# Mask and forget-gate sums built in DRAM during the projections, a reordered gate schedule, and new prices in the instruction planner

## The chip, the cores and the metric

The kernel runs on one core of a Trainium2 chip. The metric is the device time of one launch in microseconds (us). A profile of one execution gives the span of the program and the work of each engine: TensorE (PE, with its weight loads PEld), VectorE (DVE), ScalarE (ACT), GpSimd (POOL) and SyncE (SP), whose queue issues nearly all transfers.

## The reference

One layer of a hybrid encoder on a sequence of 1024 frames of 1024 channels, in float32. A token mixer with two parallel branches is followed by a gated feed-forward block; each has a residual sum and a layer norm.

```
proj = x @ w_in                # q,k,v,f of branch A; q,f,i,g of branch B; gate_a, gate_b
F    = cumsum(log_sigmoid(f_a + b_f))                    # per head, 8 heads of 64
s    = q.k / 8 + F[t] - F[s],  only keys s <= t
y_a  = softmax(s) @ v                                    # forgetting attention
y_b  = rms_norm(hgrn2(silu(q_b), f, i_b)) * sigmoid(g_b) # gated recurrence, 4 heads of 128
mix  = (sigmoid(gate_a) * (y_a @ w_pa) + sigmoid(gate_b) * (y_b @ w_pb)) @ w_o
x    = layer_norm(2**0.25 * x + mix)
out  = layer_norm(2**0.25 * x + (silu(g) * u) @ w_ff_out)   # u, g = x @ w_ff_in
```

The row constant F[t] drops out of the softmax; what attention adds to a row of scores is a term per key made from F, and a large number where a key lies ahead of the query.

## The kernel before, in words

**Arithmetic.** Every float32 product is made of three matmuls of 512 columns: each operand is split into a rounded high part (ScalarE, a copy to fp32r) and the rest as its low part (VectorE, a subtraction; `split`, line 463). The projections, gates and feed-forward products are Strassen products of seven in place of eight quarters.

**Stages.** First the values of both branches and the forget gates: `forget_gates` (627) and `forget_sums` (672) leave the gate sums, one row of 1024 numbers for each of 8 heads, in DRAM as `nf_d` (625). Then ten pairs of projections (`b_pair`, 829, for the recurrence; `qk_pair`, 814, for the queries and keys), whose weights go through the SBUF tile `box1` (594), two of its four slots for each pair in turn. Between them the recurrence of the four HGRN heads (`hgrn`, 1025). Then eight early parts of the merge gates (`gate_early`, 859: two of seven products, kept in DRAM as `part_d`; its weights in slots 0 and 1 of `box1`), eight heads of attention (`attention`, 913) and the eight late parts of the gates (`gate_late`, 870). After this come the branch projections, the output projection, and the feed-forward block.

**Attention.** A head h loads its queries and keys and two slots of `box1` (lines 922 to 925): one with the gate row on all 128 partitions, for blocks of keys fully behind the query, the other with the gate row plus the causal mask, for the blocks on the diagonal. This second slot is made in two transfers: SP loads the mask from the input, then GpSimd's queue adds the gate row to it with an accumulating DMA. Even heads use slots 2 and 3, odd heads 0 and 1. VectorE adds slot and scores and finds the row's minimum, ScalarE takes the exponential, GpSimd divides by the row sum (`pool.tensor_scalar`), TensorE transposes the blocks, they are split and multiplied with the values. The two halves of a head's result are added by another accumulating DMA of GpSimd's queue and stored to `ya_d`.

**Weights of the late gates.** Gate n takes its two raw weight tiles from the tags wr0 and wr1 (one buffer each) for even n, from the tag pf (four buffers) for odd n (line 1171). After the last gate, the branch projection loads its first weights, `wp0_0`, into wr0 and the next into wr1.

**The planner.** Nothing is issued in program order. Each call goes into `Plan` (line 62), which keeps its dependences and an estimated duration (`cost`, 145), and `schedule` (188) simulates the five queues: it always places the call that can start first and, among equals, that of the lowest rank. The steps listed in `ORDER` (34) give the first ranks, the dependences through shared tiles, and the order in which tiles of a tag are handed out. `improve` (371) repeats this 36 times, each time with ranks from the latest start that a backward pass finds (`latest`, 331), and keeps the order with the earliest simulated end. Each engine then issues its calls in that fixed order.

The prices: `LAT` is the delay in ns after which another engine sees a result, with 2400 for a transfer of SP; `OWN` the same on its own engine. A transfer of GpSimd's queue holds that engine for `SOFT` = 950 ns and lands `LANDS` + bytes / `RATE` later. A result that TensorE waits for gets `SLACK` ns on top (line 37). `MARGIN` = 1.06 stretches the durations of the other engines. Where a VectorE operation has two inputs in SBUF (`c[8]`), it is stretched while GpSimd is at work (line 268):

```
d += 0.7 * min(d, max(0.0, free["POOL"] - t))
```

`plan.behind` adds a dependence by hand: the calls recorded while it is set may not start ahead of the calls it names.

Of the kernel before, what the change touches and what calls it, by code (L numbers as in the profile page):

```python
# [7 lines left out]
F32 = mybir.dt.float32  # L8
# [4 lines left out]
ALU = mybir.AluOpType  # L13
# [3 lines left out]
P = 128  # L17
S = 1024
D = 1024
KC = D // P  # L20
NT = S // P
HA, DH = 8, 64
# [8 lines left out]
FIRST = 8  # L31
WARM = 7
ROUNDS = 36
ORDER = ("b10 00", "r0", "b20 21", "r0", "b11 01", "r0", "r0", "r0", "r0", "q0", "r1", "r1", "b12 02", "r1", "r1", "q1", "r1", "r1", "b22 23", "r2", "r2", "r2", "b13 03", "r2",
         "r2", "r2", "q2", "r3", "r3", "e0", "q3", "r3", "r3", "e1", "r3", "e2", "r3", "e3", "e4", "e5", "e6", "e7", "a0", "a1", "g0", "a2", "g1", "a3", "a4", "g2", "a5", "a6", "g3", "a7", "g4", "g5", "g6", "g7")
MARGIN = 1.06
SLACK = 400.0
SWITCH = 300.0
RING = 3
ALPHA = 2.0 ** 0.25  # L40
# [21 lines left out]
class Plan:  # L62

    LAT = {"PE": 197.0, "ACT": 131.0, "DVE": 128.0, "POOL": 66.0, "SP": 2400.0}
    OWN = {"PE": 0.0, "ACT": 0.0, "DVE": 127.0, "POOL": 60.0, "SP": 2400.0}
    SOFT, LANDS, RATE, SOONER = 950.0, 1950.0, 200.0, 1150.0
    TURN, STAY = 22.0, 300.0
    SETS = {AF.Exp: 0, AF.Ln: 0, AF.Sigmoid: 1, AF.Silu: 2}  # L70

# [73 lines left out]
    def cost(self, eng, method, outs, ins, kw):  # L145
        o = outs[0]
        n = o.free_size()
        psum = any(str(a.space).endswith("PSUM") for a in ins)
        if eng == "PE":
            dt = ins[0].dtype  # L150
            if method == "transpose":
                return 109.0
            if dt == F32:
                return 2 * max(112.0, n / 1.2 + 2)
            return n / 2.4 + 13.4 if n > 128 else 111.0
        if eng == "ACT":
            d = n / 1.2 + (52 if psum else 94) + 95 * (o.partition_size() == DH)
            if "accum_out" in kw:
                d += 93
            return d + 93 * sum(isinstance(kw.get(x), bass.AP) for x in ("scale", "bias"))  # L160
        if eng == "DVE":
            scal = sum(1 for a in ins if a.free_size() == 1 and n > 1)
            two = method in ("tensor_scalar", "tensor_copy") and not psum
            if method == "reciprocal":
                return 90.0
            if method == "tensor_tensor_scan":
                return n * 2.1 + 69
            if method == "copy_predicated":
                return n * 1.3 + 69
            if method == "bn_stats":  # L170
                n = ins[0].free_size()
            return n * (0.5208 if two else 1.0417) + 69 + 61 * min(scal, 2)
        if eng == "POOL":
            if method == "dma_start":
                return self.SOFT
            if method == "tensor_tensor" and kw.get("op") == ALU.pow:
                return 500 + 260 * n
            if method == "tensor_scalar":
                return n * 0.833 + 244
            return n * 2.35  # L180
        near = ins[0] if str(o.space).endswith("DRAM") else o
        rate = 235.0 if near.partition_size() == DH else 220.0 if tuple(ins[0].ap[0]) == (0, P) else 350.0
        return float(o.nbytes()) / rate
# [4 lines left out]
    def schedule(self, slack, wait):  # L188
# [12 lines left out]
        free = {q: 600.0 for q in self.queues}  # L201
# [19 lines left out]
        while done < len(calls):  # L221
            best = None
            for q, av in avail.items():
                for i in av:
                    t = max(free[q], ready[i])
                    ok = True
                    need = {}
                    for name in calls[i][6]:
# [10 lines left out]
                        t = max(t, sorted(slots[tag])[k][0] + 60)  # L239
# [3 lines left out]
                    if self.lands[i]:  # L243
                        t = max(t, ring[-RING])
                    if q == "SP":
                        t = max(t, under_way[-8])
# [4 lines left out]
                    r = self.rank[i]  # L251
# [6 lines left out]
            t, _, i, q = best  # L258
# [6 lines left out]
                narrow = self.narrow[i]  # L265
            if q == "DVE" and c[8]:

                d += 0.7 * min(d, max(0.0, free["POOL"] - t))
            if q == "SP":
                start = max(t + 100, dma_free)  # L270
                dma_free = start + d
# [138 lines left out]
def trunk(ctx: ExitStack, tc, a: dict, out: bass.AP):  # L410
    nc = tc.nc
    plan = Plan(tc)
# [19 lines left out]
    def take(tag, shape, name, dt=F32):  # L432
        return plan.tile(root, [P] + shape, dt, tag, name, BUFS[tag])
# [189 lines left out]


    nf_d = dram.tile([HA, S], F32, name="nf_d")

    def forget_gates():

# [200 lines left out]
    def b_pair(which, raws, banks):  # L829
        name = "b" + "".join(f"{i}{h}" for i, h in which)  # L830
        perm = which[0][0] < 2

        def put(b, hf, o, sv):
            bi, h = which[b]
            if b == 0 and hf:
                t = half("gt", f"{name}_o")
                act.activation(sv(t), o, AF.Sigmoid)
            elif bi == 0:
                t = o
                s = half("gt", f"{name}_s{hf}")  # L840
                act.activation(s, t, AF.Sigmoid)
                dve.tensor_mul(t, t, s)
            else:
                t = o
                act.activation(t, t, AF.Sigmoid)
            if bi == 1:
                act.activation(t, t, AF.Identity, scale=olb[:, h:h + 1], bias=lb[:, h:h + 1])
            if perm:
                sync.dma_start(b_d[bi, h].rearrange("p (c h t) -> p h c t", c=2, h=2)[:, hf],
                               t.rearrange("p (c t) -> p c t", c=2))  # L850
            else:
                sync.dma_start(b_d[bi, h, :, hs(hf)], t)

        strassen_pair(name, [a["w_b"][bi, h] for bi, h in which], raws, banks, perm, put)
# [58 lines left out]
    def attention(h):  # L913
        p, i = divmod(h, 2)
        me = slice(i * DH, (i + 1) * DH)
        if True:
# [4 lines left out]
            r = 2 - 2 * (h % 2)  # L921
            nfx = box1[:, r:r + 2, :].rearrange("p a (b t) -> p (a b) t", t=P)
            sync.dma_start(box1[:, r, :], nf_d[h].partition_broadcast(P))
            sync.dma_start(box1[:, r + 1, :], a["causal"])
            pool.dma_start(box1[:, r + 1, :], nf_d[h].partition_broadcast(P), accum_op=ALU.add)
            vhl = take("hl", [NT, 2, DH], f"vhl{h}", F32R)
            sync.dma_start(f(vhl), v_d[h])
            pr = []
# [96 lines left out]
    def hgrn(h, box):  # L1025
# [100 lines left out]
        for hf in range(2):  # L1126
# [20 lines left out]
            sync.dma_start(yb_d[h, :, hs(hf)], y)  # L1147
            yield

    rbox = take("v", [4, S], "rbox")  # L1150
    pairs, heads = 0, []
    for step in ORDER:
        kind, n = step[0], int(step[1])
        if kind in "bq":
            raws = [slot(box1, 2 * (pairs % 2) + i) for i in range(2)]
            banks = (("h", "h"), ("s", "s"))[pairs % 2]
            pairs += 1
            if kind == "q":
                qk_pair(n, raws, banks)
            else:  # L1160
                b_pair([(int(x[0]), int(x[1])) for x in step[1:].split()], raws, banks)
        elif kind == "e":
            gate_early(n, slot(box1, n % 2), "hs"[n % 2])
        elif kind == "r":
            if not heads or heads[-1][0] != n:
                heads.append((n, hgrn(n, rbox)))
            next(heads[-1][1])
        elif kind == "a":
            attention(n)
        else:  # L1170
            raws = [take(t, [KC, P], f"wg{n}_{i}") for i, t in enumerate((("wr0", "wr1"), ("pf", "pf"))[n % 2])]
            gate_late(n, raws, ("h", "h"))


# [748 lines left out]
```

## Time and profile before

| | |
|---|---|
| median of 3 runs | 1404.1 us (1402.64 to 1406.85) |
| the profiled execution's own time | 1403.85 us |
| its span in the profile | 1402.1 us |
| TensorE busy | 1387.0 us, 6578 matmuls |
| VectorE busy | 1154.1 us |
| ScalarE busy | 660.0 us |
| GpSimd busy | 113.8 us |
| TensorE clock granted, mean | 0.998 |
| DMA moved | 250.42 MB |

By time from the start of the span: the values and forget gates up to 87 us, projections with the HGRN heads to about 340, the early gates around 340 to 390, attention with the late gates to about 600, the branch projections to 640 and 680, the output projection to about 750, the feed-forward block from there.

A busy engine has an instruction under way; matmuls overlap in their pipeline, so one of 389 ns may follow the last after 227. A wait of TensorE shorter than the rest of the pipeline is therefore not seen as idle time. In the lists of waits a row says who waited for whose work, the total in us, how often, and the longest. In a timeline a row has its start, length, engine, line, operation, and in brackets the idle time before it and what ended it. All calls are issued from one line, 406, so work is told apart by the tiles that it writes and reads: `s` are attention's scores, `p` and `p_w` its weights, `pt`, `th`, `tl` the transposed block and its two parts, `pv` its result; `ge` and `gl_` belong to early and late gates, `T...h` and `T...l` are the two parts of a weight, `box` is `box1`, `rbox`, `hk`, `lp` belong to HGRN, `pps_` to the branch projections.

### The profile page before, as it was taken

The numbers are of one execution on the slowest core, as the hardware profiler recorded it, in microseconds if no ns is written. First come the engines' busy times: TensorE is split into PE (matmuls) and PEld (weight loads), VectorE is DVE, ScalarE is ACT, GpSimd is POOL, SyncE is SP. The second block draws the span as 40 slices with busy tenths as digits, with TensorE's granted clock in tenths as the row PEclk, the third lists the DMA queues.
The fourth block names the chain that finished last, engine by engine and source line by source line (L and its number), as shares of the span: only waits on it lengthen the run. The fifth ranks groups of instructions, "written<-read, shape, count | busy, mean of one in ns | idle before, by whom it ended". The sixth has DMA issues, their size and how long they took to land.

```text
span 1402.1 us, 19062 instructions
## 1 busy us (share of the span) xinstructions
PE 1387.0 (99%) x6578; PEld 1148.8 (82%) x6578; DVE 1154.1 (82%) x2026; ACT 660.0 (47%) x1207; POOL 113.8 (8%) x120
## 2 busy tenths in 40 slices
PE   9999999999999999999999999999999999999997
PEld 7788888888788888888887888888888888888886
DVE  8998797896498987888998889877766767999697
ACT  6545454444476776465549832233333334434430
POOL 0000001010143542000001000000000000000031
PEclk9999999999999999999999999999999999999999
DMA  7143344447897886556544636533233337977732
GB/s 273 37 177 125 108 141 151 135 136 235 275 327 236 286 240 207 178 177 222 197 147 143 208 111 224 171 120 100 99 98 110 113 113 237 337 243 231 267 133 75
DMA packets 103426, 250.42 MB, mean 179 GB/s; under 512 B 11665, under 2 KB 16913, under 8 KB 103329
## 3 DMA queue, kind: packets, MB, share of 16 engines
q1 hardware_dynamic: 100896, 242.91, 51.2%
q0 software_dynamic: 2432, 6.29, 2.5%
q8 instruction: 52, 0.85, 0.3%
q14 instruction: 46, 0.37, 0.1%
HBM read 182.77 MB, written 64.29 MB: 176 GB/s over the span
## 4 chain that ended last, share of the span: by engine, by line
PE 89%; DMA 6%; DVE 2%; ACT 1%; issue 1%; POOL 0%; SPq 0%; DVEq 0%; ACTq 0%
PE p L406 15%; PE fb L406 12%; PE fc L406 9%; PE gl_h L406 7%; PE fa L406 5%; PE b_h L406 4%; PE qk_s L406 4%; PE vx L406 4%; PE oa L406 3%; PE pps L406 3%; PE pv L406 2%; PE s L406 2%; PE ob L406 2%; PE vy L406 2%; PE pt L406 2%; PE lp L406 2%
## 5 line engine op out<-in xcount | busy, mean ns | idle before, releaser
L406 PE MATMUL p<-dp 128*128 128x512 f32 (+1 forms) x957 | 210.0, 382 | 0.0
L406 PEld LDWEIGHTS p<-dp 128*128 128x128 f32 x957 | 175.3, 188 | 34.8
L406 PE MATMUL fc<-xs,Tp 128*128 128x512 f32 x528 | 127.6, 389 | 0.0
L406 PE MATMUL fb<-xs,Tp 128*128 128x512 f32 x528 | 127.5, 389 | 0.0
L406 ACT CAST Tp<-t 128x512 fp32r<-128x512 f32 x88 | 54.5, 620 | 132.3 <-PE fb L406 59.9
L406 PEld LDWEIGHTS fc<-xs,Tp 128*128 128x128 f32 x528 | 99.1, 188 | 20.6
L406 PEld LDWEIGHTS fb<-xs,Tp 128*128 128x128 f32 x528 | 99.1, 188 | 20.6
L406 DVE TENSOR_TENSOR Tp<-t,Tp 128x512 fp32r<-128x512 f32 x88 | 60.6, 690 | 46.0 <-ACT Tp L406 45.5
L406 POOL TENSOR_TENSOR norm<-norm,few 128x1 f32<-128x1 f32 x16 | 23.4, 1464 | 796.8 <-DVE norm L406 781.7
L406 PE MATMUL fa<-x,Tp 128*128 128x512 f32 x336 | 80.9, 389 | 0.0
L406 PEld LDWEIGHTS fa<-x,Tp 128*128 128x128 f32 x336 | 63.1, 188 | 13.1
L406 ACT CAST dp<-dap 128x1024 fp32r<-128x1024 f32 (+1 forms) x42 | 40.9, 979 | 49.6 <-PE p L406 26.0
L406 DVE TENSOR_TENSOR tl<-pt,th 128x512 fp32r<-128x512 f32 (+1 forms) x96 | 52.5, 553 | 11.8 <-ACT th L406 9.6
L406 ACT CAST th<-pt 128x512 fp32r<-128x512 f32 (+1 forms) x96 | 45.6, 478 | 29.0 <-PE pt L406 24.2
L406 PE MATMUL fb<-x,Tp 128*128 128x512 f32 x240 | 57.6, 389 | 0.0
L406 DVE TENSOR_TENSOR dp<-dap,dp 128x1024 fp32r<-128x1024 f32 (+1 forms) x42 | 47.2, 1130 | 10.4 <-ACT dp L406 10.4
L406 PEld LDWEIGHTS fb<-x,Tp 128*128 128x128 f32 x240 | 45.0, 188 | 9.4
L406 DVE TENSOR_TENSOR u<-fb,p 128x512 f32<-128x512 f32 x40 | 27.6, 690 | 25.7 <-PE fb L406 25.7
L406 ACT CAST Tp<-wg_r 128x512 fp32r<-128x512 f32 x28 | 17.5, 623 | 48.1 <-PE fb L406 26.5
L406 POOL TENSOR_SCALAR p_w<-p_w,sums 128x640 f32<-128x640 f32 (+3 forms) x32 | 36.6, 1179 | 28.0 <-DVE sums L406 19.7
L406 PE MATMUL pv<-tl,vhl 128*128 128x512 f32 (+1 forms) x96 | 34.7, 365 | 1.3 <-DVE tl L406 1.3
L406 PE MATMUL pt<-ident,p_w 128*128 128x128 f32 x208 | 35.7, 274 | 0.0
(1657 smaller groups left out, 3672.0 us busy)
## 6 DMA issues: line engine op xcount, KB each, us to landing
dbp<-in_w_fo SPq DMA_DIRECT2D x45, 512.0 KB, 4.9
dap<-a_d SPq DMA_DIRECT2D x35, 512.0 KB, 4.4
wu_r<-in_w_ff SPq DMA_DIRECT2D x22, 512.0 KB, 3.7
wg_r<-in_w_ff SPq DMA_DIRECT2D x22, 512.0 KB, 3.9
a_d<-ar SPq DMA_DIRECT2D x42, 256.0 KB, 3.0
wop_r<-in_w_o SPq DMA_DIRECT2D x18, 512.0 KB, 4.0
a_d<-as SPq DMA_DIRECT2D x33, 256.0 KB, 3.4
qk_d<-qk SPq DMA_DIRECT2D x32, 256.0 KB, 3.3
```

The costliest lines, as they stand in the source:

```text
L406: getattr(q.engine, method)(*args, **kw)
```

## The change

Six edits go together.

1. A new DRAM tensor `nfc_d` holds gate row plus causal mask for each head. The new function `masked(h)` copies the mask to it inside DRAM on SP's queue, behind the last call recorded so far, and adds the gate row by an accumulating DMA of GpSimd's queue. It is called after each of the first eight projection pairs.
2. `attention` loads its second slot from `nfc_d` in one transfer; the mask load and the accumulating DMA of each head go.
3. In `ORDER`, head 0 (`a0`) stands ahead of the early gates `e6` and `e7`, and the late gate `g0` ahead of head 1. The rest of the list is the same.
4. The late gates swap their weight tags: even ones take pf, odd ones wr0 and wr1.
5. VectorE operations with two SBUF inputs are stretched by all of the time for which GpSimd is still busy. The masked copy of VectorE costs 2.4 ns an element in place of 1.3 where its innermost run is short or strided.
6. `SLACK` goes from 400 to 500 ns, SP's latency from 2400 to 2700, `LANDS` from 1950 to 4000, `RATE` from 200 to 150.

```
@@ -31,10 +31,9 @@
 FIRST = 8
 WARM = 7
 ROUNDS = 36
-ORDER = ("b10 00", "r0", "b20 21", "r0", "b11 01", "r0", "r0", "r0", "r0", "q0", "r1", "r1", "b12 02", "r1", "r1", "q1", "r1", "r1", "b22 23", "r2", "r2", "r2", "b13 03", "r2",
-         "r2", "r2", "q2", "r3", "r3", "e0", "q3", "r3", "r3", "e1", "r3", "e2", "r3", "e3", "e4", "e5", "e6", "e7", "a0", "a1", "g0", "a2", "g1", "a3", "a4", "g2", "a5", "a6", "g3", "a7", "g4", "g5", "g6", "g7")
+ORDER = ('b10 00', 'r0', 'b20 21', 'r0', 'b11 01', 'r0', 'r0', 'r0', 'r0', 'q0', 'r1', 'r1', 'b12 02', 'r1', 'r1', 'q1', 'r1', 'r1', 'b22 23', 'r2', 'r2', 'r2', 'b13 03', 'r2', 'r2', 'r2', 'q2', 'r3', 'r3', 'e0', 'q3', 'r3', 'r3', 'e1', 'r3', 'e2', 'r3', 'e3', 'e4', 'e5', 'a0', 'e6', 'e7', 'g0', 'a1', 'a2', 'g1', 'a3', 'a4', 'g2', 'a5', 'a6', 'g3', 'a7', 'g4', 'g5', 'g6', 'g7')
 MARGIN = 1.06
-SLACK = 400.0
+SLACK = 500.0
 SWITCH = 300.0
 RING = 3
 ALPHA = 2.0 ** 0.25
@@ -63,9 +62,9 @@
 
 
 
-    LAT = {"PE": 197.0, "ACT": 131.0, "DVE": 128.0, "POOL": 66.0, "SP": 2400.0}
-    OWN = {"PE": 0.0, "ACT": 0.0, "DVE": 127.0, "POOL": 60.0, "SP": 2400.0}
-    SOFT, LANDS, RATE, SOONER = 950.0, 1950.0, 200.0, 1150.0
+    LAT = {"PE": 197.0, "ACT": 131.0, "DVE": 128.0, "POOL": 66.0, "SP": 2700.0}
+    OWN = {"PE": 0.0, "ACT": 0.0, "DVE": 127.0, "POOL": 60.0, "SP": 2700.0}
+    SOFT, LANDS, RATE, SOONER = 950.0, 4000.0, 150.0, 1150.0
     TURN, STAY = 22.0, 300.0
     SETS = {AF.Exp: 0, AF.Ln: 0, AF.Sigmoid: 1, AF.Silu: 2}
 
@@ -166,7 +165,7 @@
             if method == "tensor_tensor_scan":
                 return n * 2.1 + 69
             if method == "copy_predicated":
-                return n * 1.3 + 69
+                return n * (2.4 if outs[0].ap[-1][0] > 1 or outs[0].ap[-1][1] < 3 else 1.3) + 69
             if method == "bn_stats":
                 n = ins[0].free_size()
             return n * (0.5208 if two else 1.0417) + 69 + 61 * min(scal, 2)
@@ -265,7 +264,7 @@
                 narrow = self.narrow[i]
             if q == "DVE" and c[8]:
 
-                d += 0.7 * min(d, max(0.0, free["POOL"] - t))
+                d += max(0.0, free["POOL"] - t)
             if q == "SP":
                 start = max(t + 100, dma_free)
                 dma_free = start + d
@@ -623,6 +622,7 @@
 
 
     nf_d = dram.tile([HA, S], F32, name="nf_d")
+    nfc_d = dram.tile([HA, P, S], F32, name="nfc_d")
 
     def forget_gates():
 
@@ -921,8 +921,7 @@
             r = 2 - 2 * (h % 2)
             nfx = box1[:, r:r + 2, :].rearrange("p a (b t) -> p (a b) t", t=P)
             sync.dma_start(box1[:, r, :], nf_d[h].partition_broadcast(P))
-            sync.dma_start(box1[:, r + 1, :], a["causal"])
-            pool.dma_start(box1[:, r + 1, :], nf_d[h].partition_broadcast(P), accum_op=ALU.add)
+            sync.dma_start(box1[:, r + 1, :], nfc_d[h])
             vhl = take("hl", [NT, 2, DH], f"vhl{h}", F32R)
             sync.dma_start(f(vhl), v_d[h])
             pr = []
@@ -1147,6 +1146,12 @@
             sync.dma_start(yb_d[h, :, hs(hf)], y)
             yield
 
+    def masked(h):
+        plan.behind = (len(plan.calls) - 1,)
+        sync.dma_start(nfc_d[h], a["causal"])
+        plan.behind = ()
+        pool.dma_start(nfc_d[h], nf_d[h].partition_broadcast(P), accum_op=ALU.add)
+
     rbox = take("v", [4, S], "rbox")
     pairs, heads = 0, []
     for step in ORDER:
@@ -1159,6 +1164,8 @@
                 qk_pair(n, raws, banks)
             else:
                 b_pair([(int(x[0]), int(x[1])) for x in step[1:].split()], raws, banks)
+            if pairs <= HA:
+                masked(pairs - 1)
         elif kind == "e":
             gate_early(n, slot(box1, n % 2), "hs"[n % 2])
         elif kind == "r":
@@ -1168,7 +1175,7 @@
         elif kind == "a":
             attention(n)
         else:
-            raws = [take(t, [KC, P], f"wg{n}_{i}") for i, t in enumerate((("wr0", "wr1"), ("pf", "pf"))[n % 2])]
+            raws = [take(t, [KC, P], f"wg{n}_{i}") for i, t in enumerate((("pf", "pf"), ("wr0", "wr1"))[n % 2])]
             gate_late(n, raws, ("h", "h"))
```

More of the change, by code (lines that the diff above doesn't have):

```diff
@@ L33 @@
 ROUNDS = 36
-ORDER = ("b10 00", "r0", "b20 21", "r0", "b11 01", "r0", "r0", "r0", "r0", "q0", "r1", "r1", "b12 02", "r1", "r1", "q1", "r1", "r1", "b22 23", "r2", "r2", "r2", "b13 03", "r2",
-         "r2", "r2", "q2", "r3", "r3", "e0", "q3", "r3", "r3", "e1", "r3", "e2", "r3", "e3", "e4", "e5", "e6", "e7", "a0", "a1", "g0", "a2", "g1", "a3", "a4", "g2", "a5", "a6", "g3", "a7", "g4", "g5", "g6", "g7")
+ORDER = ('b10 00', 'r0', 'b20 21', 'r0', 'b11 01', 'r0', 'r0', 'r0', 'r0', 'q0', 'r1', 'r1', 'b12 02', 'r1', 'r1', 'q1', 'r1', 'r1', 'b22 23', 'r2', 'r2', 'r2', 'b13 03', 'r2', 'r2', 'r2', 'q2', 'r3', 'r3', 'e0', 'q3', 'r3', 'r3', 'e1', 'r3', 'e2', 'r3', 'e3', 'e4', 'e5', 'a0', 'e6', 'e7', 'g0', 'a1', 'a2', 'g1', 'a3', 'a4', 'g2', 'a5', 'a6', 'g3', 'a7', 'g4', 'g5', 'g6', 'g7')
 MARGIN = 1.06
-SLACK = 400.0
+SLACK = 500.0
 SWITCH = 300.0
@@ L62 @@
 class Plan:
-    LAT = {"PE": 197.0, "ACT": 131.0, "DVE": 128.0, "POOL": 66.0, "SP": 2400.0}
-    OWN = {"PE": 0.0, "ACT": 0.0, "DVE": 127.0, "POOL": 60.0, "SP": 2400.0}
-    SOFT, LANDS, RATE, SOONER = 950.0, 1950.0, 200.0, 1150.0
+    LAT = {"PE": 197.0, "ACT": 131.0, "DVE": 128.0, "POOL": 66.0, "SP": 2700.0}
+    OWN = {"PE": 0.0, "ACT": 0.0, "DVE": 127.0, "POOL": 60.0, "SP": 2700.0}
+    SOFT, LANDS, RATE, SOONER = 950.0, 4000.0, 150.0, 1150.0
     TURN, STAY = 22.0, 300.0
@@ L168, in cost @@
             if method == "copy_predicated":
-                return n * 1.3 + 69
+                return n * (2.4 if outs[0].ap[-1][0] > 1 or outs[0].ap[-1][1] < 3 else 1.3) + 69
             if method == "bn_stats":
@@ L266, in schedule @@
             if q == "DVE" and c[8]:
-                d += 0.7 * min(d, max(0.0, free["POOL"] - t))
+                d += max(0.0, free["POOL"] - t)
             if q == "SP":
@@ L625, in trunk @@
     nf_d = dram.tile([HA, S], F32, name="nf_d")
+    nfc_d = dram.tile([HA, P, S], F32, name="nfc_d")
     def forget_gates():
@@ L923, in attention @@
             sync.dma_start(box1[:, r, :], nf_d[h].partition_broadcast(P))
-            sync.dma_start(box1[:, r + 1, :], a["causal"])
-            pool.dma_start(box1[:, r + 1, :], nf_d[h].partition_broadcast(P), accum_op=ALU.add)
+            sync.dma_start(box1[:, r + 1, :], nfc_d[h])
             vhl = take("hl", [NT, 2, DH], f"vhl{h}", F32R)
@@ L1148, in hgrn, with masked @@
             yield
+    def masked(h):
+        plan.behind = (len(plan.calls) - 1,)
+        sync.dma_start(nfc_d[h], a["causal"])
+        plan.behind = ()
+        pool.dma_start(nfc_d[h], nf_d[h].partition_broadcast(P), accum_op=ALU.add)
     rbox = take("v", [4, S], "rbox")
@@ L1161, in trunk @@
                 b_pair([(int(x[0]), int(x[1])) for x in step[1:].split()], raws, banks)
+            if pairs <= HA:
+                masked(pairs - 1)
         elif kind == "e":
@@ L1170, in trunk @@
         else:
-            raws = [take(t, [KC, P], f"wg{n}_{i}") for i, t in enumerate((("wr0", "wr1"), ("pf", "pf"))[n % 2])]
+            raws = [take(t, [KC, P], f"wg{n}_{i}") for i, t in enumerate((("pf", "pf"), ("wr0", "wr1"))[n % 2])]
             gate_late(n, raws, ("h", "h"))
```

## The prediction

> **What bounds the kernel now.** I read the page's busy lines first, then the table by stage, then what TensorE waited for.
>
> ```profile
> span 1402.1 us, 19062 instructions
> PE 1387.0 (99%) x6578; PEld 1148.8 (82%) x6578; DVE 1154.1 (82%) x2026; ACT 660.0 (47%) x1207; POOL 113.8 (8%) x120
> ...
> PE 89%; DMA 6%; DVE 2%; ACT 1%; issue 1%; POOL 0%; SPq 0%; DVEq 0%; ACTq 0%
> ```
>
> TensorE is idle for 1402.1 − 1387.0 = 15.1 us of the span. Whether "busy" also means "at its pace" is seen in the table by stage, whose columns are the stretch, its length, then busy time and instructions of each engine, the granted clock, the DMA share and GB/s:
>
> ```profile
> 87.30:340.00 252.70, 250.87 (x1293) 211.92 (x1293) 213.50 (x362) 122.30 (x245) 15.73 (x11) 1.00 0.44 147
> ...
> 365.00:560.00 195.00, 191.48 (x1054) 160.97 (x1052) 162.80 (x465) 133.99 (x298) 71.64 (x86) 1.00 0.82 261
> ...
> 806.00:1184.70 378.70, 378.61 (x1670) 313.14 (x1670) 280.56 (x429) 122.28 (x200) 0.00 (x0) 1.00 0.41 132
> 1184.70:1402.10 217.40, 209.89 (x958) 174.95 (x956) 190.17 (x252) 74.22 (x81) 17.38 (x8) 0.99 0.63 220
> ```
>
> In the feed-forward stretch one matmul of 512 columns takes 378.61 / 1670 = 0.227 us, clock 1.00, with 0.1 us idle: nothing can be won there by order. The last stretch has 7.5 us without TensorE, nearly all behind its last matmul, where the change does nothing. The change lies in the projections (87 to 340) and attention (365 to 560). What TensorE waited for between 87 and 645 us (total, times, longest):
>
> ```profile
> PE ge L406 <- ACT ge L406: 1.3, 1, 1.3
> PE pv L406 <- DVE tl L406: 1.3, 1, 1.3
> PE b_h L406 <- ACT Tb2223p7h L406: 1.2, 1, 1.2
> PE pv L406 <- ACT th L406: 0.8, 1, 0.8
> PE lp L406 <- DVE rbox L406: 0.4, 1, 0.4
> PE gl_h L406 <- DVE gl_b L406: 0.2, 1, 0.2
> PE dg L406 <- DVE qkl L406: 0.2, 1, 0.2
> ```
>
> Seven waits, together 5.4 us, are all that a better order or a less loaded queue can give back. The diff adds and removes no matmul. So the floor is the profiled execution's own 1403.85 us (1.75 outside the span) less 5.4, that is 1398.45; the median of the runs shown, 1404.1, lies 0.25 above that execution, which I add at the end. About 0.3%, 4.2 us, is what a measurement of this kernel can tell from no change: a gain that counts as one has to remove four fifths of these waits. Losses have no such bound.
>
> **The mask sums, part by part.** Before, each head loads the mask into box1 and then has GpSimd add the gates by an accumulating DMA. Afterwards the sum of each head is made in DRAM between the projections, and attention makes one load.
>
> ```profile
> q1 hardware_dynamic: 100896, 242.91, 51.2%
> q0 software_dynamic: 2432, 6.29, 2.5%
> ...
> v_d<-v SPq DMA_DIRECT2D x8, 512.0 KB, 3.0
> ...
> box<-in_causal SPq DMA_DIRECT2D x8, 512.0 KB, 7.0
> ...
> box<-nf_d POOLq DMA_DIRECT2D x8, 512.0 KB, 8.0
> ...
> ya<-ya POOLq DMA_DIRECT2D x16, 128.0 KB, 6.7
> ```
>
> Removed from attention: eight accumulates into SBUF. The GpSimd queue moved 6.29 MB in 2.5% of 1402.1 = 35 us of the sixteen engines; the eight are 4.19 MB of it, so 23 us, 2.9 each. The DMA share of 365 to 560 goes from 0.82 (160 us) to (160 − 23)/195 = 0.70, and a head's mask is there 7.0 us after its issue in place of 7.0 + 8.0. No TensorE wait above names the mask, so the direct credit is nothing; what it can do is shorten other landings.
>
> Added to the projections: eight copies inside DRAM on SP's queue and eight accumulates in DRAM on GpSimd's. Neither is in this trace. One pass at the hardware queue's rate (242.91 MB in 718 us, 338 GB/s) makes a copy 1.55 us; read and written as two passes it is 3.1. An accumulate takes 2.9 as into SBUF, or twice that if DRAM is slower. That is 8 × (1.55 to 3.1 + 2.9 to 5.8) = 36 to 71 us of DMA on top of 111 (0.44 of 252.7): a share of 0.58 to 0.72. I take the low end, as the nearest rows are for the same bytes; even the high end is below the 0.82 under which attention loses 195.0 − 191.5 = 3.5 us. Cost nothing, bounds 0 and 3.5.
>
> Each copy is hung behind the last store of its projection pair, so SP's queue gets it where the next pair's weights also go, as one issue more. On GpSimd, in order, an accumulate waits until its copy has landed (3.0 by the store's row to 7.0 by the loaded mask's), and behind it are queued the HGRN key, the powers of the norm, and through them VectorE. GpSimd is busy for 15.7 of 252.7 us there, and the sum of a head is needed only in attention. Taken as nothing, with those 7 us for one late key as the upper end where no other matmul is ready.
>
> **The planner's prices.** The whole order of all engines is a list schedule over these prices, so wrong ones turn into waits. First VectorE beside GpSimd; columns are start, length, engine:
>
> ```profile
> 456.30 0.85 POOL L406 DMA_DIRECT2D ya<-ya  x1 [3.42 <-ACT ya L406]
> 456.41 0.69 DVE L406 TENSOR_TENSOR Tgl2p6l<-wg,Tgl2p6h 128x512 fp32r<-128x512 f32 x1
> ...
> 456.88 4.06 POOL L406 TENSOR_SCALAR p_w<-p_w,sums 128x640 f32<-128x640 f32 x4
> ...
> 457.88 3.61 DVE L406 TENSOR_TENSOR Tgl2p5l<-wg,Tgl2p5h 128x512 fp32r<-128x512 f32 x1
> ...
> 462.01 0.44 PE L406 MATMUL pv<-tl,vhl 128*128 128x384 f32 x1 [1.26 <-DVE tl L406]
> ```
>
> The subtraction takes 3.61 us in place of 0.69 and ends 0.55 after GpSimd's four scalings do (460.94). The old rule allowed it 0.7 of its own length more, half a microsecond; the new one counts the whole rest of GpSimd's work. This wait of 1.3 is what the edit prices: credit 1.3, bounds 0 (the same collision elsewhere) and 1.3.
>
> The Trainium skill, SBUF — State Buffer, section "SBUF: two separate sides", calls the port pair of the two engines an exclusive lock, taken by a VectorE operation with two SBUF inputs only against a GpSimd operation that reads SBUF; a later section of the page infers that descriptor making does not block such an operation. The trace agrees on both: 3.61 beside the scalings, 0.69 beside the DMA issue at 456.30. This speaks against the edit in one point, since the new rule counts DMA issues too; by it VectorE would be priced late beside the eight accumulates.
>
> That overprice is at most 8 × 0.95 us (the planner's price of an issue) of an engine with 252.7 − 213.5 = 39 us free: nothing.
>
> The landing price of a GpSimd DMA goes from 1.95 + bytes/200 (4.6 us for 512 KB, 2.6 for 128 KB) to 4.0 + bytes/150 (7.5 and 4.9), against 8.0 and 6.7 measured. The second price matters: attention's results pass through such a DMA, and SP's in-order queue stood behind them.
>
> ```profile
> SPq L406 <- DMA ya<-ya: 48.8, 14, 6.9
> ...
> L406 DVE COPY_PREDICATED rbox<-lmask,lp 128x512 f32<-128x512 uint16 x24 | 19.6, 816 | 3.8 <-PE lp L406 3.8
> L406 DVE COPY_PREDICATED rbox<-lmask,lp_nb 128x512 f32<-128x512 uint16 x4 | 5.2, 1308 | 0.1
> ```
>
> The masked copy's new price for the dense forms, 512 × 2.4 + 69 = 1298 ns, is the 1308 of the neighbour row; before it was 735. Both edits make the plan truer; they and SLACK's extra 0.1 us are worth the three small waits in part: 0.3 of 0.8, bounds 0 and 0.8.
>
> SP's latency rises by 0.3 and SLACK by 0.1, 0.4 us more cover on each landing that a matmul hangs on. Two waits have a landing at their root, one by a store, one by a load that a table load stood behind:
>
> ```profile
> 234.69 0.69 DVE L406 TENSOR_TENSOR wb_t<-box 128x512 f32<-128x512 f32 x1 [1.14 <-DMA qk_d<-qk]
> ...
> 543.71 1.28 ACT L406 ACT_TABLE_LOAD   x1 [1.95 <-DMA sg<-gate_d]
> ```
>
> Of 1.2 and 0.8 I take 0.4 each. The lower bound for both is below nothing: with DMA added next to the first, its wait can grow as in the first rival.
>
> **ORDER.** Two early gates go behind head 0, one late gate before head 1; the late gates swap their weight buffers. The largest wait lies here:
>
> ```profile
> 377.52 1.28 ACT L405 ACT_TABLE_LOAD   x1
> ...
> 379.43 0.56 ACT L406 COPY ge<-ge 128x512 f32<-128x512 f32 x1
> ...
> 380.04 0.50 PE L406 MATMUL ge<-vs3h,Tge7p7h 128*128 128x512 f32 x1 [1.31 <-ACT ge L406]
> ```
>
> The last early gate wants the bank whose copy stands behind head 0's table load and first exponentials. With two early gates and a late one to spread around head 0, TensorE has more to run meanwhile. But the table load of 1.28 stays, and it may strike another matmul: half of 1.3, so 0.65, bounds −1.3 and 1.3.
>
> **The sum.** 1.3 + 0.3 + 0.4 + 0.4 + 0.65 = 3.05 us off: 1403.85 − 3.05 = 1400.8, plus 0.25 makes **1401.0** on the runs' scale. Next in line is what is left of the waits, 2.4 us.
>
> **The rivals.**
> Nearly all waits go: a true plan leaves only stray ones. For it: five of the seven lead back to a price that the change corrects. Against: the new order of some 2,400 matmuls has collisions that this trace cannot show. With 0 to 1 us of waits left it gives 1398.7 to 1399.7.
>
> The waits only change places: what is priced truly here is paid there, 1403 to 1405. For it: the table loads and transfers all stay.
>
> Slower, by the weights behind the last late gate. Before, gate 6 held wr0 and wr1; now gate 7 does, and the branch projection's first weights load into wr0.
>
> ```profile
> 572.50 0.33 SPq L406 DMA_DIRECT2D wp_r<-in_w_p  x1
> ...
> 588.32 0.62 ACT L406 CAST Tgl7p4h<-wg 128x512 fp32r<-128x512 f32 x1
> ...
> 590.97 0.62 ACT L406 CAST wpa_0h<-wp_r 128x512 fp32r<-128x512 f32 x1
> ...
> 598.43 0.39 PE L406 MATMUL pps_0a<-y11h,wpa_0h 128*128 128x512 f32 x1
> ```
>
> With gate 7 in wr0 the load can start only after its last split, near 589.0 in place of 572.5; with a landing like the store's to the mask's (3.0 to 7.0) and 1.3 for the split it is ready at 593.3 to 597.3, before 598.4. It decides from 1 to 5 us of further delay, which a late last split would bring; then it costs the landing and split, 4.3 to 8.3, less the 2.7 of the gate's last twelve matmuls: up to 5.6, so 1406 to 1410 with or without the credits. Against it: the planner can let gate 6 run last.
>
> Slower, by DMA among the projections: if each of the eight pairs' transfers is late like the one at 234.69, 8 × 1.2 = 10 us, about 1411. It decides where the copies delay the next pair's weights by over the 0.4 us of new cover.
>
> The added sums not being made early is no rival that costs: the planner would then wait for them with attention's loads, as before.
>
> **How the numbers follow.** Forecast 0.42 (1399.9 to 1403), nearly all gone 0.30, change of places 0.10, weights behind gate 7 0.10, DMA among the projections 0.08. Faster by over 0.3% (under 1399.9) is the second, 0.30. Slower (over 1408.3) is the last and most of the fourth, 0.16. The rest, 0.54, is the same. The range goes from 1398.2, which is the floor on the runs' scale (1398.7) less half a microsecond for runs that themselves lie from 1402.64 to 1406.85, to 1407, which leaves out some 0.16 above and 0.04 below.
>
> **What would show it.** Right: no accumulate into box1 on GpSimd in attention, DMA share there near 0.70 and near 0.6 among the projections; TensorE busy 1387 ± 1; waits of 1.5 to 4 us between 87 and 645, none behind a VectorE subtraction of over 2 us. Wrong: a wait of TensorE on wpa_0 or on a transfer of a b or qk pair, idle time above 16 us in the span, or GpSimd's key standing for microseconds behind an accumulate while HGRN's matmuls wait.

## The result, and the profile after

| | before | after |
|---|---|---|
| median of 4 runs | 1404.31 us (1402.64 to 1406.85) | 1396.87 us (1395.62 to 1397.39) |
| the profiled execution's own time | 1403.85 us | 1397.12 us |
| its span | 1402.1 us | 1395.3 us |

The ratio is 0.9944 with a 95% interval of 0.9927 to 0.9961: 7.4 us faster, clear of the 0.3%. The forecast had the sign but not the size: 1401.0, and 1396.87 lies below the range's lower end of 1398.2. It even lies below what the prediction called the floor.

The page after, its span, the busy lines and the chain:

```profile
span 1395.3 us, 19049 instructions
## 1 busy us (share of the span) xinstructions
PE 1385.7 (99%) x6578; PEld 1150.2 (82%) x6578; DVE 1152.7 (83%) x2026; ACT 661.0 (47%) x1207; POOL 111.7 (8%) x120
...
PE 99%; DVE 0%; issue 0%; ACT 0%; DVEq 0%
```

The chain that ended last had 89% on TensorE and 6% on DMA; now it has 99% on TensorE and no DMA. The matmuls are the same 6578. By stage, with the same columns as before:

```profile
87.30:340.00 252.70, 252.70 (x1305) 214.19 (x1304) 214.75 (x366) 124.06 (x248) 19.89 (x18) 1.00 0.59 180
...
365.00:560.00 195.00, 195.00 (x1078) 165.19 (x1077) 165.01 (x472) 137.23 (x302) 64.79 (x79) 1.00 0.72 241
```

TensorE has no idle time in either stretch. The DMA share of attention fell from 0.82 to 0.72, that of the projections rose from 0.44 to 0.59, as worked out. What TensorE still waits for in the whole span:

```profile
PE vy L405 <- DVE idle L405: 1.2, 1, 1.2
PE fe L405 <- ACT ep L405: 0.9, 1, 0.9
```

The first is the warm-up at the start, which was there before. All seven waits between 87 and 645 us are gone, and so is one of 0.7 at the start (`vx` on `xh`); one of 0.9 is new, in the feed-forward block.

**Where the 6.8 us of the span came from.** Idle time of TensorE went from 1402.1 − 1387.0 = 15.1 to 1395.3 − 1385.7 = 9.6: 5.5 us, of which the lists of waits give (5.4 + 0.7) − 0.9 = 5.2. The other 1.3 us came out of *busy* time, 1387.0 to 1385.7, with the same matmuls at the same clock. A matmul is shown as 389 ns and the next may start after 227, so by estimate the last 162 ns before each wait are counted as busy. Eight waits less and one more are 7 × 0.162 = 1.1 us; the kernel with put-in waits, below, bears this price out. It is not all that moves busy time: with the same 6578 matmuls it is 1384.8 us in the changed kernel under another seed (four waits) and 1387.3 in the kernel before under another seed (six). The medians add 0.7, as the profiled execution of before lay 0.46 below its median and that of after 0.25 above.

The transfers of the sums, with KB each and median us from issue to landing:

```profile
nfc_d<-in_causal SPq DMA_DIRECT2D x8, 512.0 KB, 5.4
nfc_d<-nf_d POOLq DMA_DIRECT2D x8, 512.0 KB, 6.7
...
box<-nfc_d SPq DMA_DIRECT2D x8, 512.0 KB, 6.0
```

An accumulate in DRAM lands in 6.7 us (7.6 in the kernel with the sums alone), against 8.0 into SBUF before. SP's queue stood 21.6 us behind the accumulates of attention's results, against 48.8.

### The profile page after: what moved, and what is told of

The parts are those of the page before. It is cut to its first block, busy times and chain, and to the rows that moved or that the text cites. A ratio compares the mean times of both kernels' runs of the same rounds, so it can differ in the third digit from the quotient of the medians.

```text
span 1395.3 us, 19049 instructions
## 1 busy us (share of the span) xinstructions
PE 1385.7 (99%) x6578; PEld 1150.2 (82%) x6578; DVE 1152.7 (83%) x2026; ACT 661.0 (47%) x1207; POOL 111.7 (8%) x120
## 3 DMA queue, kind: packets, MB, share of 16 engines
q1 hardware_dynamic: 101152, 247.11, 51.9%
## 4 chain that ended last, share of the span: by engine, by line
PE 99%; DVE 0%; issue 0%; ACT 0%; DVEq 0%
PE p L405 15%; PE fb L405 12%; PE fc L405 9%; PE gl_h L405 8%; PE b_h L405 6%; PE fa L405 5%; PE qk_s L405 4%; PE vx L405 4%; PE fe L405 3%; PE oa L405 3%; PE ge L405 3%; PE pps L405 3%; PE b_s L405 3%; PE vy L405 3%; PE s L405 2%; PE pv L405 2%
## 5 line engine op out<-in xcount | busy, mean ns | idle before, releaser
L405 DVE TENSOR_TENSOR dp<-dap,dp 128x1024 fp32r<-128x1024 f32 (+1 forms) x42 | 47.1, 1130 | 12.4 <-ACT dp L405 12.3
L405 POOL TENSOR_SCALAR p_w<-p_w,sums 128x640 f32<-128x640 f32 (+3 forms) x32 | 35.1, 1117 | 28.4 <-DVE sums L405 28.4
L405 DVE TENSOR_TENSOR u<-fc,u 128x512 f32<-128x512 f32 x44 | 30.2, 686 | 5.7 <-PE fc L405 5.4
```

The lines of the kernel that those rows point to most:

```text
L405: getattr(q.engine, method)(*args, **kw)
```

## The experiments

All times are ratios to the kernel before, run on the same chip in the same rounds (its medians there were 1405.0 to 1405.5 us, and 1404.3 beside the changed kernel). "Waits" is the sum of TensorE's list of waits in the profiled execution, without the 1.2 of the warm-up.

| kernel | ratio | 95% interval | waits, us |
|---|---|---|---|
| before | 1 | | 6.1 |
| before, seed 2 | 0.9957 | 0.9940 to 0.9973 | 2.4 |
| before, seed 3 | 0.9993 | 0.9980 to 1.0005 | 5.0 |
| sums in DRAM only | 0.9986 | 0.9976 to 0.9996 | 6.0 |
| ORDER and tags only | 0.9982 | 0.9971 to 0.9994 | 5.6 |
| SLACK 900 only | 0.9988 | 0.9976 to 0.9999 | 5.4 |
| VectorE rule only | 0.9979 | 0.9966 to 0.9993 | 3.7 |
| VectorE rule only, seed 2 | 0.9962 | 0.9949 to 0.9975 | 2.5 |
| landing prices only | 0.9961 | 0.9947 to 0.9976 | 2.3 |
| landing prices only, seed 2 | 0.9952 | 0.9936 to 0.9969 | 1.1 |
| all new prices | 0.9950 | 0.9938 to 0.9962 | 1.4 |
| all new prices, seed 2 | 0.9943 | 0.9925 to 0.9962 | 2.1 |
| all new prices, sums | 0.9961 | 0.9949 to 0.9974 | 2.4 |
| all new prices, ORDER | 0.9969 | 0.9957 to 0.9981 | 4.2 |
| all but the sums | 0.9969 | 0.9957 to 0.9981 | 3.0 |
| all but the sums, seed 2 | 0.9972 | 0.9962 to 0.9982 | 5.1 |
| after | 0.9944 | 0.9927 to 0.9961 | 0.9 |
| after, seed 2 | 0.9945 | 0.9929 to 0.9960 | 1.8 |

The waits are those of one execution, and they are not all that sets its time. In three of these executions (ORDER and tags only, landing prices only, VectorE rule only under seed 2) the first matmuls of 512 columns followed each other at 0.43 us in place of 0.23, up to about 10 us. These are the 5 to 10 us of the kernel before and of the one with the landing prices only:

```profile
5.00:10.00 5.00, 4.37 (x19) 3.62 (x20) 3.35 (x8) 2.92 (x6) 0.00 (x0) 1.00 0.97 330
5.00:10.00 5.00, 4.75 (x12) 3.40 (x11) 2.88 (x7) 2.54 (x5) 0.00 (x0) 1.00 0.96 328
```

There 12 matmuls stand where the other kernels have 18 to 22, some 1.5 to 2 us, which neither the waits nor the clock column (1.00) show; these executions lie 4.2, 1.5 and 2.1 us above the medians of their kernels. Why they start so is not known.

The first question was which group of edits carries the gain. Theory P says the prices, theory D the DMA that left attention, theory S the luck of a new search.

**The sums alone.** The kernel before with `nfc_d`, `masked` and the one load a head:

```
-            sync.dma_start(box1[:, r + 1, :], a["causal"])
-            pool.dma_start(box1[:, r + 1, :], nf_d[h].partition_broadcast(P), accum_op=ALU.add)
+            sync.dma_start(box1[:, r + 1, :], nfc_d[h])
```

> The kernel before with the mask sums made in DRAM alone (nfc_d, masked, one load a head); old prices, old ORDER, old weight tags. Theory P (true prices make the gain, the sums in DRAM change no wait by themselves): waits of TensorE between 87 and 645 us stay at 4 to 7 us, time 1402 to 1406. Theory D (the accumulates in attention's DMA made landings late): DMA share 365 to 560 near 0.72, waits fall to under 2 us, time 1397 to 1400.

Measured 0.9986. The DMA share of 365 to 560 is 0.72, as after, yet 6.0 us of waits remain, the largest at the first late gate:

```profile
PE gl_h L406 <- ACT Tgl0p1h L406: 2.9, 1, 2.9
```

Theory D falls: the traffic is gone and the waits are not.

**The prices alone.** Edits 5 and 6 of the change on the kernel before:

```
-SLACK = 400.0
+SLACK = 500.0
-    LAT = {"PE": 197.0, "ACT": 131.0, "DVE": 128.0, "POOL": 66.0, "SP": 2400.0}
+    LAT = {"PE": 197.0, "ACT": 131.0, "DVE": 128.0, "POOL": 66.0, "SP": 2700.0}
-    SOFT, LANDS, RATE, SOONER = 950.0, 1950.0, 200.0, 1150.0
+    SOFT, LANDS, RATE, SOONER = 950.0, 4000.0, 150.0, 1150.0
-                d += 0.7 * min(d, max(0.0, free["POOL"] - t))
+                d += max(0.0, free["POOL"] - t)
```

with SP's 2700 in `OWN` too, and the new price of the masked copy.

> The kernel before with the planner's new prices alone (SLACK, SP latency, landing of GpSimd's transfers, masked copy, VectorE beside GpSimd). Theory P: waits under 2 us and 1397 to 1400. Theory D: waits stay at 4 to 7 us, 1402 to 1406; dearer landings with the accumulates still in attention may even leave planned gaps, up to 1410.

Measured 0.9950, which the interval does not tell from the whole change. TensorE's list of waits, and attention's stretch:

```profile
PE vy L406 <- DVE idle L406: 1.2, 1, 1.2
PE x1t L406 <- ACT r L406: 0.6, 1, 0.6
PE gl_h L406 <- ACT Tgl0p1h L406: 0.4, 1, 0.4
PE oa L406 <- ACT Top4h L406: 0.2, 1, 0.2
PE s L406 <- DVE soft L406: 0.2, 1, 0.2
```

```profile
365.00:560.00 195.00, 194.42 (x1073) 164.54 (x1072) 161.09 (x468) 135.67 (x301) 75.13 (x86) 1.00 0.82 261
```

With all the accumulates still in attention and the DMA share at 0.82, TensorE is idle for 0.6 us where it was for 3.5. This is theory P.

**ORDER and tags alone.**

```
-... "e6", "e7", "a0", "a1", "g0", "a2" ...
+... 'a0', 'e6', 'e7', 'g0', 'a1', 'a2' ...
-... (("wr0", "wr1"), ("pf", "pf"))[n % 2] ...
+... (("pf", "pf"), ("wr0", "wr1"))[n % 2] ...
```

> The kernel before with the new ORDER and the swapped weight tags of the late gates alone. Theory P: 1402 to 1406, though the wait of the last early gate on ScalarE (1.3 us) may go. Theory D: the same. Theory S (every new search of the planner gives a new set of accidental waits, and the gain is a draw): anything from 1397 to 1408, and so for all four kernels, in no relation to the edit.

Measured 0.9982 with 5.6 us of waits, two of which are of the sort that the prediction credited to ORDER and to the landings:

```profile
PE b_h L405 <- ACT Tb2223p7h L405: 1.8, 1, 1.8
PE s L405 <- ACT ge L405: 1.4, 1, 1.4
```

A wait on an early gate's copy did not go with ORDER. Behind the wait of 1.8 us the granted clock fell, as it does behind longer ones below:

```profile
240.00:245.00 5.00, 4.18 (x14) 3.46 (x15) 5.00 (x9) 3.35 (x12) 1.84 (x1) 0.69 0.28 107
```

This execution took 1406.65 us, the slowest of twelve.

**All but the sums.** The changed kernel with the two old transfers a head and without `masked`.

> The changed kernel without the sums in DRAM: each head again loads the mask and accumulates into SBUF; prices, ORDER and tags are new. Theory P: within 1.5 us of the changed kernel, 1396 to 1399. Theory D: 1401 to 1406, with waits that lead back to late transfers in attention.

Measured 0.9969, some 3.5 us slower than the whole change: between the two theories, and slower than the prices alone. Its largest wait lies in neither attention nor the early gates, but in the branch projections:

```profile
PE pps_0a L405 <- ACT pu L405: 1.5, 1, 1.5
```

The kernel is repeated under another seed below.

**One price at a time.** First the rule for VectorE beside GpSimd:

```
-                d += 0.7 * min(d, max(0.0, free["POOL"] - t))
+                d += max(0.0, free["POOL"] - t)
```

> The kernel before with one price changed: a VectorE operation with two SBUF inputs is stretched by all of GpSimd's remaining time. Theory P1 (this is the price that matters): waits on VectorE's parts (tl, soft) go, together under 3 us between 87 and 645 us, time 1398 to 1400. Theory P2 (the landings matter): waits of 4 us and more stay, 1401 to 1406. In both the collisions themselves (VectorE subtractions stretched beside GpSimd, 6.8 us in sum before, 6.4 in the changed kernel) should stay in the trace.

Measured 0.9979. The waits on VectorE fell to 0.2 each; one of 2.9 on ScalarE's copy of an early gate was left.

Then the landings, SP's latency in `LAT` and `OWN` and the price of GpSimd's transfers:

```
-    LAT = {"PE": 197.0, "ACT": 131.0, "DVE": 128.0, "POOL": 66.0, "SP": 2400.0}
+    LAT = {"PE": 197.0, "ACT": 131.0, "DVE": 128.0, "POOL": 66.0, "SP": 2700.0}
-    SOFT, LANDS, RATE, SOONER = 950.0, 1950.0, 200.0, 1150.0
+    SOFT, LANDS, RATE, SOONER = 950.0, 4000.0, 150.0, 1150.0
```

> The kernel before with only the landing prices changed (SP 2400 to 2700, GpSimd's transfers 1950 + bytes/200 to 4000 + bytes/150). Theory P2: waits under 3 us, 1398 to 1400. Theory P1: the wait on VectorE at 460 us or its like stays, 1401 to 1406. A wait of TensorE over 1.8 us should show a granted clock near 0.5 to 0.7 for some 3.5 us behind it, as in the two kernels that have such a wait (0.66 in 5 us, 0.69 in 5 us), and add 1.5 to 2 us of its own.

Measured 0.9961. Head 0 has hardly any wait left, and the wait on VectorE stayed, as P1 and P2 would each have it for their part:

```profile
PE pt L406 <- DVE tl L406: 1.4, 2, 1.1
PE s L406 <- DVE soft L406: 0.2, 1, 0.2
PE s L406 <- ACT ge L406: 0.2, 1, 0.2
```

Then margin without truth:

```
-SLACK = 400.0
+SLACK = 900.0
```

> The kernel before with SLACK 900 in place of 400 and all other prices old: margin without truth. Theory M (any added cover in front of TensorE does it): waits under 2 us, 1397 to 1400. Theory T (only the right price at the right operation does it): half a microsecond hides the waits of 0.2 to 0.4 but not those of 1.2 and more, which come from errors of 2 to 3 us; 1400 to 1404.

Measured 0.9988, with 5.4 us of waits, one of them 2.2 at the early gates. In this one draw, half a microsecond more in front of every matmul does not stand in for the new prices.

**The draw of the search.** `improve` varies the slack of its rounds by a seeded generator. Other seeds change nothing else:

```
-        vary = np.random.default_rng(1)
+        vary = np.random.default_rng(2)
```

All prices, seed 2:

> The kernel before with all new prices, and another seed of the planner's search. Theory P: the gain is in the prices, so another draw keeps it: 1396 to 1399.5, waits under 2 us. Theory S (the gain is a draw): anything from 1397 to 1406.

Measured 0.9943. The kernel before, seeds 2 and 3:

> The kernel before with another seed of the planner's search, nothing else. It sizes the draw: theory P (the old prices are why TensorE waits) expects waits of 3 to 7 us again between 87 and 645 us and 1400 to 1406; theory S (the kernel before had a bad draw) expects some seed under 1399.

> As the second seed: theory P 1400 to 1406, theory S under 1399 for one of the two.

Measured 0.9957 and 0.9993. So the draw is worth up to 6 us under the old prices (4.8 by the medians), and the kernel before had the worst of three. Theory S wanted a seed under 1399, which neither gave (1400.2 and 1404.3), but there is something in it: the three draws average 0.9983, so by estimate some 2.3 us of the gain are the bad luck of the kernel before. Under the new prices both seeds lie within 1 us. The changed kernel, seed 2:

> The changed kernel with another seed. Theory P: 1396 to 1399, as with the prices alone under both seeds (1397.9 and 1397.1). If the sums in DRAM and the new ORDER added something of their own to the prices, it would have to be faster than those by over 1 us in both seeds.

Measured 0.9945, no faster than the prices alone, and under this seed the intervals do not tell it from the old prices (0.9957).

With draws of that size one run of a single price proves little, so both were repeated under seed 2:

> Landing prices alone, second seed (first: 0.9961). The kernel before has 1.0, 0.9957 and 0.9993 under its three seeds. If the landings alone carry the gain, 0.994 to 0.997 again; if it takes all prices, anything from 0.995 to 1.0.

Measured 0.9952, with 1.1 us of waits.

> The rule for VectorE beside GpSimd alone, second seed (first: 0.9979, with one wait of 2.9 us at head 0). If this rule carries the gain, 0.994 to 0.997; if it takes all prices, anything from 0.995 to 1.0.

Measured 0.9962, with 2.5. Neither is told from the old prices under the same seed (0.9957). That the landings are the larger part is possible; two draws of each don't settle the shares. The masked copy's price, SLACK 500 and the two landing prices apart were not run.

**Do the sums and ORDER add anything to the prices?** All but the sums, seed 2:

> The changed kernel without the sums in DRAM, second seed. If the sums carry something of their own, 1399.5 to 1402 again (first seed: 0.9969 of the kernel before). If that was a draw, 1396 to 1399, as the prices alone.

Measured 0.9972, so the loss without them is hardly a draw. The other two corners, prices with sums and prices with ORDER:

> The new prices with the sums in DRAM, old ORDER and weight tags. If the sums gain by themselves (less DMA in attention), under 0.9935 of the kernel before, 1395 to 1396. If they only undo a loss that the new ORDER or tags bring without them, 0.994 to 0.9955, as the prices alone.

Measured 0.9961: no gain of their own.

> The new prices with the new ORDER, the accumulates still in attention, and the old weight tags. If ORDER brings the loss where the sums are missing, 0.9965 to 0.9975; if the swapped tags do (the branch projection's first weights behind the last late gate, where one of the two slower kernels has a wait of 1.5 us), 0.994 to 0.9955.

Measured 0.9969: the loss comes with ORDER where the accumulates are still in attention; the tags are not needed for it. One of its waits near head 0, and what ScalarE did just before:

```profile
387.38 0.50 PE L405 MATMUL pv<-th,vhl 128*128 128x512 f32 x1 [1.23 <-ACT ya L405]
```

```profile
386.74 0.59 ACT L405 COPY ya<-pv 128x512 f32<-128x512 f32 x1 [4.17 <-DMA part_d<-ge]
```

TensorE wants the bank of head 0's first result; ScalarE's copy out of it stood 4.2 us for the store of an early gate's part, whose buffer it takes over. The seed 2 kernel without the sums has the same at the same place:

```profile
388.12 0.50 PE L405 MATMUL pv<-th,vhl 128*128 128x512 f32 x1 [1.16 <-ACT ya L405]
```

```profile
387.48 0.59 ACT L405 COPY ya<-pv 128x512 f32<-128x512 f32 x1 [2.04 <-DMA part_d<-ge]
```

With head 0 ahead of the last two early gates, their stores land among head 0's and 1's loads and, without the sums, their accumulates. In the changed kernel no matmul there waits. Beside the prices, sums and ORDER together are worth nothing that can be measured. Either one alone measures slower than the prices, ORDER by 2.7 to 3.7 us and the sums by 1.5 to 2.5, of which the second is within the noise. For ORDER these stores are a cause seen in two kernels (1.2 us in each); the first kernel without the sums has its wait of 1.5 us elsewhere, as shown above.

**All kernels together.** The eight with all the new prices lie between 0.9943 and 0.9972. Of the six with the old ones (three seeds, sums only, ORDER only, SLACK 900) five lie between 0.9982 and 1, and one, seed 2, at 0.9957. The new prices shift the field as a whole; how much of the 7.4 us is theirs and how much the draw of the kernel before can be told only roughly.

**The price of a wait.** The changed kernel, with copies of a 128 x 128 constant put on ScalarE's queue at nine places of the feed-forward stretch, so that TensorE runs out of split weights:

```
+                for _k in range(self.late.get(i, 0)):
+                    self.act.copy(*self.pad)
...
+    plan.act, plan.pad = nc.scalar, (ones, ident)
...
+        if c > 3 and c % 2 == 0:
+            plan.late[len(plan.calls)] = (40, 50, 60, 70, 75, 80, 85, 90, 100)[c // 2 - 2]
```

> The changed kernel with 40 to 100 extra copies of a 128 x 128 constant (0.2 us each by their form) put on ScalarE's queue ahead of nine places of the feed-forward stretch, 38 us apart, so that TensorE runs out of split weights for a while at some of them. It prices a wait. Without a reaction of the clock each microsecond of wait costs that microsecond and 0.16 us of pipeline; with it, waits from some length between 1.5 and 3 us on are followed by about 3.5 us at half the clock, another 1.7 us each.

The copies took longer in a row than expected and gave waits of 7 to 27 us, with a granted clock of 0.50 to 0.65 in the 4 us behind each. The same with 20, 21, 22, 23, 24, 25, 27, 30 and 34 copies (each of the two kernels ran once):

> As the earlier kernel with extra copies on ScalarE, now 20 to 34 of them: by that kernel a copy takes 0.33 us in a row and TensorE has some 6 us of split weights ahead, so waits of 0.5 to 5 us are expected. Clock theory: the granted clock falls to half for about 3.5 us behind every wait over some 3 us, behind some of the waits of 1.8 to 2.9 us (four of five seen so far) and behind none under 1.5. Without it the clock stays at 1.00 behind all.

TensorE's timeline at seven of the waits (start, length, instructions, in brackets the wait), and the table of the 4 us behind the first six of these:

```profile
875.36 3.01 PE L408 MATMUL fb<-xs,Tp 128*128 128x512 f32 x12 [1.08 <-DVE u L408]
898.76 1.65 PE L408 MATMUL fb<-x,Tp 128*128 128x512 f32 x3 [3.40 <-DVE u L408]
937.06 3.01 PE L408 MATMUL fc<-xs,Tp 128*128 128x512 f32 x12 [2.01 <-DVE u L408]
...
1018.78 1.39 PE L408 MATMUL fc<-xs,Tp 128*128 128x512 f32 x5 [2.67 <-DVE u L408]
1060.47 3.00 PE L408 MATMUL fc<-xs,Tp 128*128 128x512 f32 x12 [3.33 <-DVE u L408]
1103.16 4.57 PE L408 MATMUL fc<-xs,Tp 128*128 128x512 f32 x12 [4.32 <-DVE u L408]
1148.72 5.46 PE L408 MATMUL fc<-xs,Tp 128*128 128x512 f32 x12 [5.64 <-DVE u L408]
```

```profile
875.36:879.36 4.00, 4.00 (x18) 3.29 (x19) 4.00 (x8) 0.62 (x1) 0.00 (x0) 1.00 0.59 176
898.76:902.76 4.00, 4.00 (x11) 3.21 (x12) 3.13 (x5) 0.00 (x0) 0.00 (x0) 0.60 0.56 189
937.06:941.06 4.00, 4.00 (x18) 3.29 (x19) 3.86 (x7) 1.30 (x3) 0.00 (x0) 1.00 0.08 7
...
1018.78:1022.78 4.00, 4.00 (x18) 3.29 (x19) 3.86 (x7) 1.29 (x3) 0.00 (x0) 1.00 0.02 1
1060.47:1064.47 4.00, 4.00 (x18) 3.29 (x19) 3.87 (x7) 1.30 (x3) 0.00 (x0) 1.00 0.02 6
1103.16:1107.16 4.00, 4.00 (x11) 3.13 (x12) 3.64 (x6) 0.67 (x2) 0.00 (x0) 0.57 0.00 0
```

After the waits of 3.40 and 4.32 only 11 matmuls fit into 4 us where 18 do at full clock, all of it shown as busy: 7 × 0.227 = 1.6 us lost beside the wait itself. After 3.33, a fifteenth of a microsecond less, nothing is lost. After the longest, 5.64, twelve matmuls took 5.46 us in place of 3.01, so 2.4 are lost there. The whole kernel adds up: its span is 1429.0 − 1395.3 = 33.7 us longer than the changed kernel's. The list of waits is longer by 28.4 − 2.1 = 26.3 us and by 11 waits, 11 × 0.162 = 1.8, and the clock took, by estimate, 1.6 + 1.6 + 2.4 = 5.6; together 33.7.

In the kernels above the clock fell behind waits of 1.8 (ORDER and tags only), 2.4 (before, seed 3), 2.9 (sums only) and 2.9 us (VectorE rule only), and stayed behind one of 2.2 (SLACK 900). The seed 3 kernel, in the 10 us around its wait:

```profile
380.00:385.00 5.00, 2.32 (x8) 1.74 (x9) 2.46 (x14) 3.20 (x7) 0.00 (x0) 0.86 0.96 317
385.00:390.00 5.00, 5.00 (x25) 3.80 (x24) 4.53 (x21) 3.71 (x9) 2.08 (x4) 0.80 1.03 414
```

So a wait costs its own length and 0.16 us; from 1.8 us on it may cost another 1.6 or more. Length alone does not decide it, as 1.8 lost the clock and 3.33 did not; what else does is open. The Trainium skill, TensorE: Matmul & The Clock Gate, Part 1, gives an idle window of about 3.4 us, free-running, for the drop; that it depends on more than the length agrees with 3.33 and 3.40, that 1.8 and 2.4 us are enough does not follow from a whole idle window, and there the measurement decides.

## Why the prediction was right or wrong, point by point

**The bound** was read rightly: no matmul changed, and the gain is TensorE's waits.

**The size was wrong in two steps.** Of the 4.2 us between the forecast of 1401.0 and the result, 2.4 are idle time (5.5 us went, 3.05 were credited), 1.3 are busy time that the prediction took as fixed, and 0.5 the medians: 0.25 was added for a median that lay above the profiled execution, and after the change it lay 0.25 below. The credits are taken one by one below; the landings were the term mis-sized most. The second step is the floor.

**The floor was wrong**, and it set the range's lower end. "Seven waits, together 5.4 us, are all that a better order or a less loaded queue can give back" left out the 1.1 us of pipeline that those waits hide in busy time, though the front part gives both durations, 389 and 227 ns, and says that short waits don't show; it left out the 0.7 at the start, though the edits reprice the whole kernel; and it took one execution's waits for those of all.

Of the prediction's signs of being right, TensorE busy 1387 ± 1 and waits of 1.5 to 4 us did not come: 1385.7, and none between 87 and 645 us. The prediction had also no term for the draw of the search, and the one draw before was a bad one; that part of the gain is luck.

**The mask sums** were costed at nothing, and the run with them alone gives 0.9986 with as many waits as before. The shares came out as bounded: 0.72 (0.70 forecast) and 0.59 (0.58 to 0.72).

**VectorE beside GpSimd.** Credit 1.3, and that wait is gone. But the collisions are not: operations of VectorE on two tiles of 512 columns (TENSOR_TENSOR) that took over 0.8 us number 11 before and 13 after, with 6.8 and 6.4 us above their 0.69. One of them, after:

```profile
430.00 2.15 DVE L405 TENSOR_TENSOR wg<-wg 128x512 f32<-128x512 f32 x1
430.22 1.38 POOL L405 TENSOR_SCALAR p_w<-p_w,sums 128x1024 f32<-128x1024 f32 x1
```

The plan now knows of them and lets no matmul hang on one. No wait shows harm from its overprice of DMA issues.

**The landings** were the term sized worst: 0.4 of 1.2 and 0.4 of 0.8, for the 0.4 us of new cover. With the landing prices alone the waits fell from 6.1 to 2.3 us, and under the other seed from 2.4 to 1.1. The prediction had GpSimd's 2.6 against 6.7 us in front of it, an error of 4 us, and credited it with a part of 0.3. The new price does change what it is about: SP's queue stood 48.8 us behind the accumulates of attention's results (34.1 under seed 2), and 12.9 (12.3) with the landing prices alone. The prediction also looked at what each wait named last (a table load, an exponential) and not at what had pushed those late: ScalarE's copies of the early gates stood behind landings of their own stores, as the list of ScalarE's waits shows; these are the kernel before, the one with the VectorE rule alone, and the one with the landing prices alone:

```profile
ACT ge L406 <- DMA part_d<-ge: 10.4, 6, 3.4
```

```profile
ACT ge L406 <- DMA part_d<-ge: 11.7, 4, 4.6
```

```profile
ACT ge L406 <- DMA part_d<-ge: 2.9, 5, 1.0
```

The second has TensorE's wait of 2.9 us on just this copy. These stores are SP's (3.4 us to land), whose price rose by only 0.3 us. In the kernel before, the copies' waits lie between 355 and 377 us, where GpSimd's queue starts no transfer (330.77 and 382.55 are the nearest), so its error of 4 us did not hold these copies directly. Which of the two landing prices removed the waits was not run and stays open.

**ORDER** was credited 0.65 for the early gate's wait. Alone it leaves one of that sort (1.4), and beside the new prices the three kernels that have it without the sums are slower than the prices alone. No run supports the credit; with the prices alone no such wait is left.

**The rivals.** "Nearly all waits go" (0.30) is what happened, priced some 2 us too high by the same floor and medians. The last gate's weights: the plan split product p4 of gate 7 before p5 and p6, so wr0 was free early and the first branch weight was split at 584.0, 4.6 us ahead of its first matmul:

```profile
574.88 0.62 ACT L405 CAST Tgl7p4h<-wg 128x512 fp32r<-128x512 f32 x1 [1.66 <-PE gl_h L405]
...
583.42 0.62 ACT L405 CAST wpa_0h<-wp_r 128x512 fp32r<-128x512 f32 x1
```

```profile
588.69 0.39 PE L405 MATMUL pps_0a<-y11h,wpa_0h 128*128 128x512 f32 x1
```

DMA among the projections delayed nothing: 252.70 of 252.70 us busy.

## What to carry to other kernels

Where a planner fixes the order of a kernel that one engine bounds, check its prices against the trace's durations and landings: all the new prices gave 0.9950 and 0.9943 under two seeds, where one draw with 0.5 us of slack everywhere gave 0.9988. Count a visible wait with the pipeline it hides and, from about 1.8 us on, with the clock it may lose. Before crediting an edit to a searched schedule, run other seeds: here they moved the unchanged kernel by up to 6 us.

## What the runs showed of the hardware

The clock can drop behind a single wait of 1.8 to 2.9 us inside an otherwise full stretch (granted 0.57 to 0.65 in the 4 us behind), and the time lost, some 1.6 us behind the waits of 3.40 and 4.32, is shown as busy. The kernel before spread from 1400.7 to 1409.9 us in one set of 17 runs, the new prices under seed 2 from 1396.7 to 1399.9 in 6; that waits make the spread is not shown, as the kernel without the sums under seed 2, with 5.1 us of waits, kept 12 runs between 1399.8 and 1402.3. And copies in DRAM were cheaper than bounded, by an estimate from two totals: the hardware queue's share went from 51.2% of 1402.1 us to 51.9% of 1395.3, some 6 us for eight copies, 0.8 each, where the prediction's lower end was 1.55. The rounding of the shares alone moves this by up to 0.2 each, and what other transfers gained or lost is in it.
